# HGRN2 scores on the diagonal and between pair neighbours: two sets of keys in place of parity sums

## The chip, the cores and the metric

The kernel runs on one core of one Trainium2 chip, as one program. The metric is the device time of one execution in microseconds (us); lower is better. The engines go by the names of the profile: PE (TensorE matmuls), PEld (TensorE weight loads), DVE (VectorE), ACT (ScalarE), POOL (GpSimd) and SP, whose queue issues nearly all transfers from memory. Each engine takes its instructions strictly in the order in which the program wrote them; semaphores order them between engines.

## The reference

Two encoder layers over 512 tokens of width 1024 in float32. Each layer is a mixer and an expert-choice feed-forward network (FFN) with 16 experts. The mixer projects the normalised input onto nine groups of 512 columns, runs four retention heads and four HGRN2 heads of 128 channels, and projects back. What matters here is the HGRN2 head, in both directions over the sequence:

```
S_t = diag(f_t) S_{t-1} + k_t v_t^T        o_t = S_t^T q_t        k_t = 1 - f_t
scores[t, s] = sum_d q[t, d] k[s, d] prod_{s < r <= t} f[r, d]
```

The score of a token with itself is `sum_d q k`, with the keys of both directions added, since both include the diagonal. The score of a token with its neighbour in the same pair (tokens 2j and 2j+1) has a single forget factor, `sum_d q[t] k[s] f[t]`, from the forward direction for the later token and from the backward one for the earlier.

## The kernel before, in words

Channels lie on the 128 partitions and tokens along the free axis. For a head `c`, `K[:, hh]` holds the keys of both directions (2 x 512), `F[:, hh]` the forget factors and `self.q[:, c]` the queries. Scores inside a block of 128 tokens are made level by level: level width m = 1 joins tokens within a pair, and LEVELS = 2, 4, ..., 64 join ever larger neighbours. `ascend(c, n, m)` moves a head up one level: it multiplies half of the keys by forget products (DVE, L551, "kv" below), copies them to a tile for the next level's matmuls (two ACT copies, L531, "keys"), multiplies half of the queries (DVE, L556, "qv") and makes the products for the next level (POOL, L561). At each level four matmuls (L604) make scores of four blocks of 128 tokens, and DVE puts those that belong to the level into `AT` under a mask (L606).

The heads go in two pairs, (0, 1) and (2, 3). `hgrn_pair` is a generator: for both heads the keys of the two directions are added (POOL, L568) and Q = F q is made (DVE, L569); then the products for the diagonal and the neighbour (DVE, L579 and L580), which are split into a rounded part (ACT, L582) and a rest (POOL, L583); then `ascend(c, 0, 1)`; then four matmuls with `parity`, a matrix of alternating ones and zeros, sum the products over the channels (PE, L591), and DVE multiplies the sums by a mask of pairs (L594). After that come the levels, the transposes of the keys ("turn", L619), the states between blocks (L644, L647, L650) and the outputs (L663, copied out by ACT, L632). The float32 matmuls (L604, L644, L663, L721) each show as two loads and two matmuls in the trace; those of the reduced form fp32r (L465, L591) show as one.

The generator is woven into the projections by `lead`. A projection `proj(n, ...)` yields 16 times, after every six matmuls (L465; 128 x 512 each). At every yield a credit rises by the projection's budget B; while it is over zero, the generator is advanced to its next yield, whose value is taken off the credit. So the place of each HGRN step among PE's matmuls is fixed when the program is written:

```
credit += budget
while side is not None and credit > 0.0:
    cost = next(side, None)
    if cost is None:
        break
    credit -= cost
```

The budgets are 1.0, 1.2, 1.0, 0.9 and 2.2 for projections n = 3 to 7. In order they make `v2`, then `rq` and `rk`, which are rotated head by head in the last four yields of their projection (two ACT copies of half the partitions, L513 and L514; DVE L515; POOL L516; DVE L523, added one head late), then `rv` and `rg`. The yields' values stand in `COSTS`, with 1.2 for the Q step, 0.4 for a turn, 1.0 for states and 0.5 for outputs. Retention (L720, L721, its ACT copies L723, its states by the same L644) is added to the generator from n = 7 on. The weights of a projection are split into a rounded part and a rest as they are needed (ACT L436, DVE or POOL L438). The FFN's matmuls are L1145 and L1265; its weights are read from memory into the 22 slots of 1 MB that the mixer gives back when it is done, by DMAs that SP issues in one order.

Of the kernel before, what the change touches and what calls it, by code (L numbers as in the profile page):

```python
# [10 lines left out]
F32R = mybir.dt.float32r  # L11
BF = mybir.dt.bfloat16
U8 = mybir.dt.uint8
AF = mybir.ActivationFunctionType
OP = mybir.AluOpType

P = 128
S = 512
D = 1024
NT = S // P  # L20
# [45 lines left out]
class Kernel:  # L66
# [156 lines left out]
    def more_consts(self):  # L223
        nc, a, cp = self.nc, self.a, self.cp
        q = nc.gpsimd
        pt = self.pb()
        nc.tensor.transpose(pt[:, :24], self.rows, self.ident[:24, :24])
        for i in range(2):
            nc.tensor.transpose(pt[:, 24 + 8 * i:32 + 8 * i], self.rows2[:, self.apart(0, i)], self.ident[:8, :8])
        self.cols = cp.tile([P, 40], F32, name="cols")  # L230
        nc.vector.tensor_copy(self.cols[:, :24], pt[:, :24])

        nc.vector.tensor_copy(self.cols[:, 24:].rearrange("p (j two) -> p two j", two=2),
                              pt[:, 24:40].rearrange("p (two j) -> p two j", two=2))
        self.lmask = cp.tile([P, len(LEVELS), P], U8, name="lmask")
        lm = self.tmp4([len(LEVELS), P])
        q.dma_start(lm, a["lmask"])
        nc.gpsimd.tensor_copy(self.lmask, lm)
        for nm, shape in (("slots", [CAP]), ("sel", [NH + 1 + NT]), ("two", [P]), ("fold", [NE]), ("dec_k", [NH, 2])):
            t = cp.tile([P] + shape, F32, name=nm)  # L240
            setattr(self, nm, t)
            q.dma_start(t, a[nm])

        turns = self.tmp2(shape=(P + 2,))
        nc.gpsimd.memset(turns, 0.0)
        nc.gpsimd.memset(self.view(turns, 1, [[2, P // 2 + 1]]), 1.0)
        self.parity = cp.tile([P, P + 2], F32R, name="parity")
        nc.gpsimd.tensor_copy(self.parity, turns)
        self.selR = cp.tile([P, NH + 1], F32R, name="selR")
        nc.gpsimd.tensor_copy(self.selR, self.sel[:, :NH + 1])  # L250
        u = self.tmp2(shape=(P,))
        q.dma_start(u, a["upto"])
        self.upto, self.all = cp.tile([P, P], BF, name="upto"), cp.tile([P, P], BF, name="all")
        nc.gpsimd.tensor_copy(self.upto, u)
        nc.gpsimd.memset(self.all, 1.0)
        self.lower_bound()
# [159 lines left out]

    WAITS, RATE = (1, 1, 2), 0.7
    EARLY = 5
    COSTS = (1.2, 1.3, 0.65, 1.9)
    BUDGET = (1.0, 1.2, 1.0, 0.9, 2.2, 1.3)  # L420
    GROUPS = (4, 5, 6, 7, 0, 1, 2, 3, 8)

# [111 lines left out]
    def hgrn_pair(self, hp):  # L534

        nc, v = self.nc, self.nc.vector
        heads = (2 * hp, 2 * hp + 1)
        F, K = self.F[hp], self.K[hp]  # L540
        Q = self.slot([2, 2, S])
        AT, T, Tn, kt, B = {}, {}, {}, {}, {}

        def ascend(c, n, m):

            q0, k0, J = Q[:, c % 2], K[:, c % 2], S // (2 * m)
            t, ts = T[c]
            to = t.offset
            kv = self.view(k0, m, [[S - m, 2], [2 * m, J], [1, m]])
            tk = bass.AP(tensor=t.tensor, offset=to, ap=[list(t.ap[0]), [ts + 1, 2], [2, J], [0, m]])  # L550
            v.tensor_tensor(kv, kv, tk, op=OP.mult)  # L551
            if 2 * m < P:
                kt[c] = self.level_keys(B[c][:, n % 2], k0, 2 * m)
            qv = self.view(q0, 0, [[S + m, 2], [2 * m, J], [1, m]])
            tq = bass.AP(tensor=t.tensor, offset=to + 1, ap=[list(t.ap[0]), [ts - 1, 2], [2, J], [0, m]])
            v.tensor_tensor(qv, qv, tq, op=OP.mult)  # L556
            dst, ds = (Tn[c], J) if n % 2 == 0 else (F[:, c % 2], S)
            te = bass.AP(tensor=t.tensor, offset=to, ap=[list(t.ap[0]), [ts, 2], [2, J]])
            td = bass.AP(tensor=t.tensor, offset=to + 1, ap=[list(t.ap[0]), [ts, 2], [2, J]])
            dv = bass.AP(tensor=dst.tensor, offset=dst.offset, ap=[list(dst.ap[0]), [ds, 2], [1, J]])  # L560
            nc.gpsimd.tensor_tensor(dv, te, td, op=OP.mult)  # L561
            T[c] = (dst, ds)

        for c in heads:
            hh = c % 2
            B[c] = self.slot([4, S])
            AT[c], Tn[c] = B[c][:, 2], B[c][:, 3]
            nc.gpsimd.tensor_tensor(AT[c], K[:, hh, 0], K[:, hh, 1], op=OP.add)  # L568
            v.tensor_tensor(Q[:, hh], F[:, hh], self.q[:, None, c].to_broadcast([P, 2, S]), op=OP.mult)  # L569
            T[c] = (F[:, hh], S)  # L570
            yield 1.2
        X = {}
        for c in heads:


            q0, k0, x = Q[:, c % 2], K[:, c % 2], B[c][:, :2]
            X[c] = self.slot([2, 2, S], F32R)
            flat = lambda t: t.rearrange("p (j two) -> p j two", two=2)
            v.tensor_tensor(self.view(x, 0, [[2, S // 2], [S + 1, 2]]), flat(AT[c]), flat(self.q[:, c]), op=OP.mult)  # L579
            v.tensor_tensor(self.view(x, S, [[2, S // 2], [1 - S, 2]]), self.view(k0, 1, [[2, S // 2], [S - 1, 2]]),  # L580
                            self.view(q0, 0, [[2, S // 2], [S + 1, 2]]), op=OP.mult)
            nc.scalar.activation(X[c][:, 0], x, AF.Copy)  # L582
            nc.gpsimd.tensor_tensor(X[c][:, 1], x, X[c][:, 0], op=OP.subtract)  # L583
            yield self.COSTS[0]
        for c in heads:
            ascend(c, 0, 1)
            yield self.COSTS[1]
        for c in heads:
            sc = self.pb()
            for i in range(4):  # L590
                nc.tensor.matmul(sc, lhsT=self.parity[:, 1 - i % 2:1 - i % 2 + P], rhs=X[c][:, i // 2, i % 2],  # L591
                                 start=(i == 0), stop=(i == 3))
            AT[c] = AT[c].rearrange("p (b t) -> p b t", b=NT)
            v.tensor_tensor(AT[c], sc.rearrange("p (b t) -> p b t", b=NT),  # L594
                            self.two[:, None, :].to_broadcast([P, NT, P]), op=OP.mult)
            self.put(X[c])
            yield self.COSTS[2]
        for n, m in enumerate(LEVELS, 1):
            for c in heads:
                q0 = Q[:, c % 2]  # L600
                sc = self.pb().rearrange("p (b t) -> p b t", b=NT)
                for b in range(NT):
                    qv = self.view(q0, b * P, [[2 * m, P // (2 * m)], [S + m, 2], [1, m]])
                    nc.tensor.matmul(sc[:, b], lhsT=kt[c][:, b * P:(b + 1) * P], rhs=qv, start=True, stop=True)  # L604
                ascend(c, n, m)
                v.copy_predicated(AT[c], self.lmask[:, None, n - 1].to_broadcast([P, NT, P]), sc)  # L606
                yield self.COSTS[3]

        W = {}
        for c in heads:  # L610
            part = lambda x: x[:, :3 * P].rearrange("p (b t) -> p b t", b=3)
            W[c] = [part(B[c][:, 0]), part(B[c][:, 1]), part(F[:, c % 2, 0]), part(F[:, c % 2, 1])]
        for c in heads:
            hh = c % 2
            for d in range(2):
                pk = self.pb().rearrange("p (b t) -> p b t", b=NT)
                for i in range(3):
                    b = i + 1 - d
                    nc.tensor.transpose(pk[:, i], K[:, hh, d, b * P:(b + 1) * P], self.ident)  # L619
                nc.scalar.activation(W[c][d], pk[:, :3], AF.Copy)  # L620
            yield 0.4
        for c in heads:
            t, ts = T[c]
            self.states(W[c], self.v2, c, lambda d, b: t[:, d * ts + b:d * ts + b + 1])
            yield 1.0
        for c in heads:
            hh = c % 2
            if self.oh is None:
                self.oh = self.slot([NH, S])
            po = self.tile_outputs(W[c], self.v2, c, AT[c], Q[:, hh, 0, :3 * P], Q[:, hh, 1, P:])  # L630
            yield 0.5
            nc.scalar.activation(self.oh[:, c], po, AF.Copy)  # L632
            self.put(B[c])
        self.put(F, K, Q)
# [70 lines left out]
    def retention(self):  # L705
# [5 lines left out]
        nc.gpsimd.dma_start(dec_q, self.a["dec_q"])  # L711
        W, X, AT = {}, {}, {}

# [656 lines left out]
```

## Time and profile before

| what | value |
|---|---|
| three runs | 1638.16, 1639.77, 1640.24 us; median 1639.77 |
| the profiled execution | 1637.67 us, of which the span of its instructions is 1635.8 us |
| PE busy, PE weight loads busy | 94%, 58% of the span |
| DVE, ACT, POOL busy | 41%, 29%, 14% |
| mean granted TensorE clock | 0.977 of full speed |

The profile is of one execution, and its times are read against its own 1637.67 us. A busy share of PE counts matmuls from start to modelled end, which overlap; idle time of PE is listed as waits, with the instruction that ended each. The granted clock is given as a share of full speed (1.00 is 2.4 GHz, 0.50 is 1.2 GHz).

### The profile page before, as it was taken

To read this page: it belongs to the slowest core of one execution; us is meant where nothing else is said; L and a number is where in the kernel's file an instruction comes from. 1 tells how busy PE (TensorE), PEld (TensorE's weight loads), DVE (VectorE), ACT (ScalarE), POOL (GpSimd) and SP (SyncE) were. 2 spreads that over 40 slices of the span, in tenths; PEclk is the share of its full clock that TensorE was granted. 3 is DMA by queue.
4 is the path that set the end of the run, shared out by engine and by line. 5 is a ranking of instruction groups with operands and counts; after the bars stand their busy time and mean duration, and the time that the engine had idled before them with its cause. 6 is when DMAs were issued, how large, how long until landed. Compare 5 with 4: busy or idle time off the path is not lost. (4 is left out here: it accounts for less than half of the span.)

```text
span 1635.8 us, 19932 instructions
## 1 busy us (share of the span) xinstructions
PE 1531.0 (94%) x7970; PEld 954.9 (58%) x7970; DVE 664.4 (41%) x1107; ACT 474.9 (29%) x889; POOL 229.3 (14%) x201
## 2 busy tenths in 40 slices
PE   7989899969999999999999899999699999999986
PEld 6878798754354534533478787977444445444333
DVE  5378945561121312212254889464511122212113
ACT  4334444542221200200343434455322202112003
POOL 3042542100000000011021344430000000000201
PEclk9999999989999999999999999999799999999998
DMA  7211132577999999999941211317699999999997
GB/s 262 75 53 52 52 124 78 211 303 301 427 425 426 427 426 427 426 427 427 400 176 51 78 41 64 123 52 258 273 385 427 420 427 426 427 427 426 426 426 275
DMA packets 94605, 464.53 MB, mean 284 GB/s; under 512 B 7904, under 2 KB 16288, under 8 KB 48432
## 3 DMA queue, kind: packets, MB, share of 16 engines
q1 hardware_dynamic: 93040, 458.35, 69.0%
q0 software_dynamic: 1472, 4.90, 0.8%
q8 instruction: 63, 1.03, 0.2%
q14 instruction: 30, 0.25, 0.0%
HBM read 459.03 MB, written 4.19 MB: 283 GB/s over the span
## 5 line engine op out<-in xcount | busy, mean ns | idle before, releaser
L1145 PE MATMUL pj<-s,s 128*64 128x512 f32 x2048 | 478.8, 599 | 19.2 <-DMA s<-in_w_up_dram 13.9
L465 PE MATMUL pj<-s,s 128*128 128x512 f32 x1728 | 426.7, 401 | 12.9 <-DVE s L438 8.6
L465 PEld LDWEIGHTS pj<-s,s 128*128 128x128 f32 x1728 | 324.2, 192 | 82.7 <-DVE s L438 11.6
L1145 PEld LDWEIGHTS pj<-s,s 128*64 128x64 f32 x2048 | 173.3, 137 | 279.6 <-issue 203.3
L1265 PE MATMUL pb<-s,t 128*64 128x512 f32 x896 | 197.8, 594 | 5.4 <-ACT t L1183 2.7
L1272 POOL TENSOR_TENSOR s<-s,s 128x1024 f32<-128x1024 f32 x8 | 18.7, 2362 | 872.1 <-DVE s L1205 823.5
L1265 PEld LDWEIGHTS pb<-s,t 128*64 128x64 f32 x896 | 66.0, 137 | 126.8 <-issue 110.8
L1193 DVE SCALAR_TENSOR_TENSOR t<-pb,sm,t 128x512 fp32r<-128x512 f32 (+1 forms) x34 | 24.5, 719 | 242.5 <-ACT t L1192 241.0
L1205 DVE TENSOR_TENSOR s<-s,pb 128x512 f32<-128x512 f32 (+1 forms) x112 | 67.3, 661 | 130.0 <-PE pb L1200 130.0
L909 PE MATMUL pj<-s,s 128*128 128x512 f32 x384 | 96.6, 400 | 3.4 <-DVE s L796 2.9
L438 DVE TENSOR_TENSOR s<-s,s 128x1024 fp32r<-128x1024 f32 x62 | 84.3, 1383 | 37.8 <-ACT s L436 37.6
L1110 DVE COPY sm<-pb 128x2 f32<-128x2 f32 x16 | 2.5, 159 | 210.9 <-PE pb L1107 210.9
L909 PEld LDWEIGHTS pj<-s,s 128*128 128x128 f32 x384 | 69.3, 189 | 20.7 <-DVE s L796 4.6
L1192 ACT ACTIVATE t<-pb,sm 128x512 fp32r<-128x512 f32 (+1 forms) x34 | 22.5, 662 | 195.4 <-PE pb L1265 183.2
L1088 PEld LDWEIGHTS pb<-t,t 128*128 128x128 f32 x512 | 64.9, 199 | 17.3 <-issue 15.0
L1121 ACT ACTIVATE t<-pb 128x512 fp32r<-128x512 f32 x16 | 9.6, 601 | 221.0 <-PE pb L1119 221.0
L436 ACT ACTIVATE s<-s 128x1024 fp32r<-128x1024 f32 x72 | 73.4, 1048 | 0.0
L1088 PE MATMUL pb<-t,t 128*128 128x256 f32 x512 | 69.8, 293 | 3.2 <-DVE t L1072 2.4
L1200 PE MATMUL pb<-t,t 128*128 128x512 f32 (+1 forms) x256 | 66.7, 401 | 0.1
L556 DVE TENSOR_TENSOR s<-s,s 128x512 f32<-128x512 f32 x56 | 59.3, 1059 | 13.4 <-PE pb L604 13.4
L1200 PEld LDWEIGHTS pb<-t,t 128*128 128x128 f32 x256 | 44.7, 188 | 33.0 <-issue 19.4
L531 ACT ACTIVATE s<-s 128x256 f32<-128x256 f32 x96 | 35.3, 415 | 93.8 <-DVE s L551 93.5
(237 smaller groups left out, 1541.2 us busy)
## 6 DMA issues: line engine op xcount, KB each, us to landing
s<-in_w_gate_dram SPq DMA_DIRECT2D x124, 1024.0 KB, 19.5
s<-in_w_up_dram SPq DMA_DIRECT2D x124, 1024.0 KB, 19.6
s<-in_w_down_dram SPq DMA_DIRECT2D x112, 1024.0 KB, 19.6
s<-in_w_in_dram SPq DMA_DIRECT2D x34, 1024.0 KB, 5.9
s<-in_w_down_dram SPq DMA_DIRECT2D x32, 512.0 KB, 9.4
s<-in_w_out_dram SPq DMA_DIRECT2D x8, 1024.0 KB, 4.8
s<-in_x_dram SPq DMA_DIRECT2D x8, 512.0 KB
s<-in_w_gate_dram SPq DMA_DIRECT2D x8, 512.0 KB, 5.6
```

Source lines behind the costliest of these rows:

```text
L436: nc.scalar.activation(wh, src, AF.Copy)
L438: e.tensor_tensor(low, src, wh, op=OP.subtract)
L465: nc.tensor.matmul(pg[c], lhsT=lhsT, rhs=rhs, start=(k == 0 and m == 0), stop=(k == ND - 1 and m == 2))
L531: self.nc.scalar.activation(kv[:, :, e], src, AF.Copy)
L556: v.tensor_tensor(qv, qv, tq, op=OP.mult)
L909: nc.tensor.matmul(po, lhsT=x, rhs=w, start=(k == 0 and i == 0), stop=(k == ND - 1 and i == 2))
L1088: nc.tensor.matmul(pt[:, i], lhsT=x[:, tt, k % 2::2], rhs=oh[:, tt], start=(tt == 0 and x is self.picked[u][0]), stop=(tt == NT - 1 and x ...
L1145: nc.tensor.matmul(pg[n + 2 * f][e * CAP:(e + 1) * CAP], lhsT=self.xe[:, k, at + e * CAP:at + (e + 1) * CAP], rhs=w[e][:, f * 512:(f + 1) ...
L1193: v.scalar_tensor_tensor(yL[0][:, cs], py, gate, yH[0][:, cs], op0=OP.mult, op1=OP.subtract)
L1200: nc.tensor.matmul(pc, lhsT=ohT[:, tt * P:(tt + 1) * P], rhs=y[:, cs], start=(y is yH[0]), stop=(y is yL[0]))
L1205: v.tensor_tensor(dst, dst, pc, op=OP.add)
L1265: nc.tensor.matmul(py[f][e * CAP:(e + 1) * CAP], lhsT=hT[:, k, e * CAP:(e + 1) * CAP], rhs=W[e][:, k2, f * 512:(f + 1) * 512], start=(k == ...
```

## The change

The products, their split, and the matmuls with `parity` go, and so does `parity` itself. Instead each head gets two sets of keys in a tile `near`: set i serves the queries of parity i. At a token of the same parity it holds the sum of both directions' keys (POOL writes it there, strided), and at the other it holds the neighbour's key, already multiplied by its forget factor: `ascend(c, 0, 1)` makes it, and a new ACT copy brings it to `near`. Eight float32 matmuls per head (four blocks, two parities; 128 x 128 keys, 64 queries at every other token) then make the scores, and DVE multiplies by the same mask of pairs. One entry of COSTS (1.2, for the products) falls away, so that everything after it comes at an earlier yield.

```diff
-        turns = self.tmp2(shape=(P + 2,))
-        nc.gpsimd.memset(turns, 0.0)
-        nc.gpsimd.memset(self.view(turns, 1, [[2, P // 2 + 1]]), 1.0)
-        self.parity = cp.tile([P, P + 2], F32R, name="parity")
-        nc.gpsimd.tensor_copy(self.parity, turns)
...
-    COSTS = (1.2, 1.3, 0.65, 1.9)
+    COSTS = (1.3, 0.65, 1.9)
...
+        near = self.slot([2, 2, S])
+        flat = lambda t: t.rearrange("p (j two) -> p j two", two=2)
         for c in heads:
             hh = c % 2
             B[c] = self.slot([4, S])
-            AT[c], Tn[c] = B[c][:, 2], B[c][:, 3]
-            nc.gpsimd.tensor_tensor(AT[c], K[:, hh, 0], K[:, hh, 1], op=OP.add)
+            AT[c], Tn[c] = B[c][:, 2].rearrange("p (b t) -> p b t", b=NT), B[c][:, 3]
+            nc.gpsimd.tensor_tensor(self.view(near[:, hh], 0, [[2, S // 2], [S + 1, 2]]), flat(K[:, hh, 0]), flat(K[:, hh, 1]), op=OP.add)
             v.tensor_tensor(Q[:, hh], F[:, hh], self.q[:, None, c].to_broadcast([P, 2, S]), op=OP.mult)
             T[c] = (F[:, hh], S)
             yield 1.2
-        X = {}
         for c in heads:
-            q0, k0, x = Q[:, c % 2], K[:, c % 2], B[c][:, :2]
-            X[c] = self.slot([2, 2, S], F32R)
-            flat = lambda t: t.rearrange("p (j two) -> p j two", two=2)
-            v.tensor_tensor(self.view(x, 0, [[2, S // 2], [S + 1, 2]]), flat(AT[c]), flat(self.q[:, c]), op=OP.mult)
-            v.tensor_tensor(self.view(x, S, [[2, S // 2], [1 - S, 2]]), self.view(k0, 1, [[2, S // 2], [S - 1, 2]]),
-                            self.view(q0, 0, [[2, S // 2], [S + 1, 2]]), op=OP.mult)
-            nc.scalar.activation(X[c][:, 0], x, AF.Copy)
-            nc.gpsimd.tensor_tensor(X[c][:, 1], x, X[c][:, 0], op=OP.subtract)
+            ascend(c, 0, 1)
+            nc.scalar.activation(self.view(near[:, c % 2], 1, [[S - 1, 2], [2, S // 2]]),
+                                 self.view(K[:, c % 2], 1, [[S - 1, 2], [2, S // 2]]), AF.Copy)
             yield self.COSTS[0]
         for c in heads:
-            ascend(c, 0, 1)
+            sc = self.pb().rearrange("p (b t) -> p b t", b=NT)
+            for b in range(NT):
+                for i in range(2):
+                    nc.tensor.matmul(sc[:, b, i::2], lhsT=near[:, c % 2, i, b * P:(b + 1) * P],
+                                     rhs=self.q[:, c, b * P + i:(b + 1) * P:2], start=True, stop=True)
+            v.tensor_tensor(AT[c], sc, self.two[:, None, :].to_broadcast([P, NT, P]), op=OP.mult)
             yield self.COSTS[1]
-        for c in heads:
-            sc = self.pb()
-            for i in range(4):
-                nc.tensor.matmul(sc, lhsT=self.parity[:, 1 - i % 2:1 - i % 2 + P], rhs=X[c][:, i // 2, i % 2],
-                                 start=(i == 0), stop=(i == 3))
-            AT[c] = AT[c].rearrange("p (b t) -> p b t", b=NT)
-            v.tensor_tensor(AT[c], sc.rearrange("p (b t) -> p b t", b=NT),
-                            self.two[:, None, :].to_broadcast([P, NT, P]), op=OP.mult)
-            self.put(X[c])
-            yield self.COSTS[2]
+        self.put(near)
```

## Rows read from the trace of the kernel before

**Rows 1.** By stage: PE, PEld, DVE, ACT, POOL busy us; granted clock; DMA share, GB/s.
```profile
82.80:240.00 157.20, 148.30 (x829) 127.63 (x828) 118.27 (x145) 64.18 (x123) 68.97 (x62) 0.96 0.19 66
...
310.00:850.00 540.00, 509.01 (x2603) 260.33 (x2602) 147.98 (x313) 120.78 (x233) 19.25 (x11) 0.98 0.94 387
```

**Rows 2.** PE's waits, 75 to 240 us (layer 0): total, times, longest.
```profile
PE pb L591 <- POOL s L583: 4.5, 3, 2.2
PE pb L604 <- ACT s L531: 2.4, 1, 2.4
PE pj L465 <- DVE s L438: 2.0, 1, 2.0
```

**Rows 3.** PE's waits, 890 to 1070 us (layer 1); the L604 row repeats rows 2.
```profile
PE pb L591 <- POOL s L583: 4.6, 3, 2.3
...
PE pj L465 <- DVE s L438: 2.2, 1, 2.2
PE pb L591 <- ACT s L582: 1.0, 1, 1.0
```

**Rows 4.** Busy time in stretches at half clock (columns as in rows 1).
```profile
96.80:103.60 6.80, 4.84 (x12) 3.26 (x12) 6.80 (x5) 0.90 (x3) 5.43 (x3) 0.50 0.22 84
...
195.80:199.20 3.40, 3.40 (x12) 2.82 (x12) 3.40 (x3) 1.00 (x3) 3.05 (x2) 0.50 0.00 0
```

**Rows 5.** The chain that ended last, layer 1: start, us, what.
```profile
917.47 2.74 PE pj L465 x12
920.21 0.89 PE pb L604 x8
```

**Rows 6.** Groups by line and shape: busy us, mean ns, idle before.
```profile
L604 PEld LDWEIGHTS pb<-s,s 128*128 128x128 f32 x384 | 51.6, 194 | 10.3 <-ACT s L531 6.5
...
L531 ACT ACTIVATE s<-s 128x256 f32<-128x256 f32 x96 | 35.3, 415 | 93.8 <-DVE s L551 93.5
...
L583 POOL TENSOR_TENSOR s<-s,s 128x1024 fp32r<-128x1024 f32 x8 | 22.1, 2789 | 18.3 <-ACT s L582 14.8 <-issue 3.4
...
L1107 PEld LDWEIGHTS pb<-sm,t 128*64 128x64 f32 x256 | 15.2, 138 | 7.5 <-issue 7.5
...
L495 ACT ACTIVATE s<-pj 128x512 f32<-128x512 f32 x16 | 9.5, 592 | 19.2 <-PE pj L465 19.1
...
L723 ACT ACTIVATE s<-pb,dec_k 128x384 f32<-128x384 f32 x16 | 8.4, 578 | 6.9 <-PE pb L720 6.9
```

**Rows 7.** Timeline of the first pair's start, layer 0: start, us, engine, line.
```profile
79.58 2.58 DVE L569 TENSOR_TENSOR s<-s,s 128x1024 f32<-128x1024 f32 x2 [11.62 <-ACT s L477]
...
87.50 2.53 POOL L568 TENSOR_TENSOR s<-s 128x512 f32<-128x512 f32 x2
88.81 2.18 DVE L579 TENSOR_TENSOR s<-s,s 128x512 f32<-128x512 f32 x1 [6.65 <-POOL s L568]
...
93.72 0.63 PE L591 MATMUL pb<-s,parity 128*128 128x512 f32 x2
...
98.76 3.47 POOL L561 TENSOR_TENSOR s<-s 128x512 f32<-128x512 f32 x2
...
99.81 1.52 DVE L551 TENSOR_TENSOR s<-s,s 128x512 f32<-128x512 f32 x1
...
102.71 0.68 DVE L551 TENSOR_TENSOR s<-s,s 128x512 f32<-128x512 f32 x1
```

**Rows 8.** Timeline of one head's rotation in `rq`, layer 0.
```profile
145.15 0.59 ACT L513 ACTIVATE t<-pj 64x512 f32<-64x512 f32 x1
...
146.38 0.69 DVE L515 TENSOR_TENSOR s<-pj,t 128x512 f32<-128x512 f32 x1 [2.19 <-ACT t L514]
146.42 1.29 POOL L516 TENSOR_TENSOR t<-t,t 128x512 f32<-128x512 f32 x1 [1.57 <-ACT t L514]
146.98 1.28 DVE L523 TENSOR_TENSOR s<-s,t 128x512 f32<-128x512 f32 x1
```

More of the change, by code (lines that the diff above doesn't have):

```diff
@@ L606, in hgrn_pair @@
                 v.copy_predicated(AT[c], self.lmask[:, None, n - 1].to_broadcast([P, NT, P]), sc)
-                yield self.COSTS[3]
+                yield self.COSTS[2]
         W = {}
```

## Prediction

> **What bounds the kernel now.** I read the stages first [rows 1]. In the FFN the DMA engines are busy for 94% of the time, and its transfers can only begin when the mixer gives its slots back: during the HGRN stage the DMA share is 0.19. So a microsecond gained or lost in the mixer moves the whole FFN after it and comes out at the end one for one; the stage to look at is 82.8 to 240 us, and its like in layer 1. There PE is busy for 148.3 of 157.2 us while DVE is for 118.3 and POOL for 69.0. PE sets the time, and what it waits for is next.
>
> PE's waits in the two stages are few [rows 2, 3]: for the rest of the products (POOL L583) before the parity matmuls, 4.5 and 4.6 us; for a split that is late on DVE (L438), 2.0 and 2.2; for the products' rounded part (L582), 1.0 in layer 1; and, apart from the changed code, for level keys (L531), 2.4 each. Each batch of waits is followed by a stretch at half the clock, 1.2 GHz [rows 4]: in the 6.8 us one PE is busy for 4.84, and half of that, 2.4, is lost; in the 3.4 us ones, of which there are two per layer, it is busy throughout and loses 1.7. So the changed steps cost PE, beyond their own work, 6.5 + 7.8 of waiting and 2 x (2.4 + 1.7) of clock: 22.5 us in all. The level-key wait with its clock is another 4.1 per layer.
>
> **PE's own work.** Six L465 take half of 2.74 us [rows 5], so 0.228 each. The parity matmuls have the same form and size: four per head, 0.91. They go. The new ones are eight float32 matmuls per head, so 16 loads and 16 matmuls, of which the trace has the same kind with 128 moving columns: eight pairs in 0.89, 0.111 a pair [rows 5]. Do 64 columns halve that? A load of 128 columns lasts 194 ns and one of 64 lasts 138 [rows 6]: 0.87 ns per column, so 128 columns stream for about 0.11 us, the whole of a pair. The loads alone fill the pace, and I take 16 x 0.111 = 1.78 per head. That is 0.87 more than before, and with eight heads in two layers **+7.0**. If the moving columns set the pace it would be 0.89 per head and the change nothing (-0.2 in all); if load and matmul did not overlap, 0.111 + 0.056, 2.67 per head and +14.1.
>
> The Trainium skill says ("TensorE: Matmul & The Clock Gate", The mechanism) that a load overlaps a matmul in flight only when their row groups differ; by that rule the full 128-row loads here would be serial and the term +14.1. The trace speaks against it: eight pairs with loads of 0.11 and matmuls of the same length would then take 1.8 us, not 0.89 [rows 5].
>
> **Where the scores now stand.** I worked the credits through by hand. Before, the first pair's scores follow yields 8 and 9 of the `v2` projection, after 48 and 54 L465; two steps of 1.2 are gone, so now both heads' scores come together after yield 6, after 36. For the second pair the savings add up. Before: its Q steps at yield 16 of `rq` and 1 of `rk`, its scores at yield 7 of `rk`. After: Q at yields 13 and 14 of `rq`, `ascend` with the new copy at 15 and 16, both scores at yield 1 of `rk`. These are the four yields at which `rq` is rotated. Behind PE's scores stand all the matmuls of `rk`, so a wait there is lost.
>
> **First pair.** PE reaches the scores 12 x 0.228 = 2.7 us before the 93.72 at which it began the parity matmuls [rows 7], so at 91.0. The key sums (POOL L568) end at 90.03. While they run, DVE stands nearly still: L579 took 2.18, against some 1.1 that remained after POOL was done. Beside POOL's L561 a kv takes 1.52, and 0.68 without it [rows 7]. So the first head's kv ends at about 91.2, two key copies of 0.415 and the new copy of about 0.59 (L495, the same count) [rows 6] at 92.6, and PE waits 1.6. The second head's qv and kv follow qv of the first; near is complete about 95.0, PE is free at 92.6 + 1.78 = 94.4, and waits 0.6. With one half-clock stretch of 1.7 that makes 4.0 (2.2 without it, 5.6 with two). In layer 1, where the waits were 1.0 longer, I take 5.0. **+9.0.**
>
> **Second pair, the largest term.** Let zero be the moment when PE has the first head of `rq`. It then has one head's outputs left (L663, 20 pairs, 2.2) and four times six L465 (1.37): it reaches the scores at 7.7, and the second head's at 9.5. The others have more. ACT needs 1.2 per rotated head, DVE 0.69 for L515, POOL 1.29 for L516, DVE 0.67 to 1.28 for L523 [rows 8], in the order written: head 0, Q and sum, head 1, Q and sum, head 2, kv/keys/qv/copy, head 3, kv/keys/qv/copy. The last kv waits on DVE for 4 L515, 3 L523, 2 Q (1.29 each [rows 7]) and 2 of kv and qv: 2.8 + 2.0 + 2.6 + 1.4, and 0.7 for itself, from 1.3 on: 10.8, and with keys and copy 12.2. So even with POOL out of the way PE waits 2.7. POOL is not out of the way: L523 took 0.6 more beside L516 [rows 8], L579 1.1 more beside L568. Four L516, two sums and one L561 come to 5.2 + 2.5 + 1.7 = 9.4; if all of that holds DVE up, less 2.8 while L515 reads PSUM, which it did beside L516 in its usual 0.69, the last copy is done at 18.8, and 1.2 later still because ACT rotates head 3 only after the first head's copy: a wait of up to 10.5. The nearest rows show DVE held for most of an overlap, so I take 8.5 for both heads. After it I put 2.5 for the clock (1.7 for one stretch, up to 4). 11.0 per layer, **+22.0**; at the lower bound 4.4 per layer.
>
> The Trainium skill ("SBUF — State Buffer", Who interferes with whom) calls the port that DVE shares with POOL an exclusive lock for operations with two SBUF inputs. By it the wait would be the 10.5 and the term 26; the trace agrees for L523 and L579, and does not for kv beside L561, which went on at less than half pace.
>
> **What else shifts.** The level-key wait at the end of `rk` goes: the step whose keys were late was issued after all four rotations and used three yields on. Now the steps there are issued at yields 13 and 15, with four yields to their use. From the first rotated head on, the later kv has three L515, three L523 and one step of some 2.1 before it on DVE, after 1.2 on ACT: 9.9 with itself, its keys at 10.7. PE is there after six times 1.37 and three levels of 0.89, at 10.9. That is just in time, and for a DVE that is behind I give back 1.5 per layer (0 to 4.1, as before): -8.2 + 3.0, **-5.2**. The HGRN steps now end three yields before the end of `rv`, so retention's first yield holds the first head's keys and, with nothing between, its states, which need two ACT copies of 0.578 [rows 6] after the transposes: 1.4 per layer, **+2.8**, from nothing to 3. The rest I cost at nothing. The products' DVE work, and POOL's L583 (2.79 each [rows 6]), come off engines that nothing else waits for but the waits already counted. The matrix `parity` was made by POOL early in layer 0. Two slots fewer are held and one more; weights of projections are not among PE's waits [rows 2, 3].
>
> **Sum.** +7.0 - 22.5 + 9.0 + 22.0 - 5.2 + 2.8 = +13.1, on 1637.67 some 1650.8. The median of the runs is 2.1 above the profiled execution, so I say **1653**. With my own bounds on the second pair and on what remains at other places, the likeliest case spans about 1642 to 1664.
>
> **Rivals.**
> - The second pair's keys come in time. In its favour: POOL is rid of two L583 per pair, 5.6 us, and DVE of four products. Against it: four rotations stand in the same queues, and even the free chain is 2.7 late. At 1 us per layer in place of 11 the sum is -6.9: 1633. It decides from a second-pair cost of 4.4 per layer downwards: there the sum is about zero. Chance 0.14 for faster.
> - The waits move and balance. The second pair at its lower bound, 4.4 per layer, gives -0.1: no change, 1640. Or the FFN takes up the loss, against which the idle DMA in the mixer speaks. Chance 0.10.
> - Loads that don't overlap: +7.1 more, 1660. Pairs of 0.111 with loads as long speak against it. Chance 0.08.
> - The forecast, slower by the second pair's wait: 0.68.
>
> Slower 0.76, same (within 0.2%, about what a measurement of this kernel can tell from no change) 0.10, faster 0.14. The range reaches from the balance to a second pair at its upper bound with a clock loss of 4 (+7 above the forecast) and part of serial loads: **1638 to 1666**.
>
> **What would show it.** New matmuls at 0.11 a pair; no POOL waits of parity matmuls; the longest PE waits of the stage on the new ACT copy, two per pair, in the second pair next to L513 to L523; half-clock stretches after them; retention's first states waiting for L723; the wait for L531 at 195 us gone or shorter. Wrong it would be if the second pair's scores run without a wait of several microseconds, or if pairs with 64 columns take half the time.

## The result and the profile after

The changed kernel takes 1680.39 us (median of four runs, 1676.39 to 1682.72) where the kernel before takes 1639.08 on the same chip (four runs, 1638.16 to 1640.24): a ratio of 1.0249, 95% interval 1.0227 to 1.0271. That is slower, as forecast, but by 41 us in place of 13, and outside the range. The profiled execution after has a span of 1679.4 us, 43.6 longer than that of before.

First, by stage, where the 43.6 us are. The marks are the first matmuls of each stage in the two traces, and the end.

| stage | before, us | after, us | difference |
|---|---|---|---|
| start to the end of the layer 0 mixer's projections | 298.0 | 311.4 | +13.4 |
| output projection and selection, layer 0 | 72.3 | 72.5 | +0.2 |
| FFN, layer 0 | 451.3 | 459.1 | +7.8 |
| mixer, layer 1 | 285.5 | 297.9 | +12.4 |
| output projection and selection, layer 1 | 72.3 | 72.5 | +0.2 |
| FFN, layer 1, to the end | 456.4 | 465.9 | +9.5 |

The mixers lose 25.8 us and the FFNs 17.3. Nothing in the prediction has the second number: it let the FFN only follow the mixer.

The mixer first. PE's waits in layer 0 of the kernel after, 75 to 260 us (total, times, longest):
```profile
PE pb L579 <- ACT s L572: 9.9, 4, 5.9
PE pj L459 <- POOL s L432: 1.5, 1, 1.5
PE pb L630 <- ACT s L709: 1.0, 1, 1.0
PE pj L459 <- DVE s L509: 0.8, 1, 0.8
PE pb L590 <- ACT s L525: 0.6, 1, 0.6
```
L579 are the new score matmuls, L572 is the new ACT copy; the waits for the products are gone, and of the 2.4 for level keys of [rows 2] the 0.6 of the last row is left. In layer 1 the first row reads (900 to 1090 us; the four others are the same):
```profile
PE pb L579 <- ACT s L572: 11.4, 4, 5.9
```
The timeline shows the two pairs of layer 0 (start, us, engine, line; in brackets the idle time before it and what ended that):
```profile
92.59 2.00 PE L579 MATMUL pb<-s,s 128*128 128x64 f32 x16 [0.90 <-ACT s L572]
...
95.42 3.67 PE L579 MATMUL pb<-s,s 128*128 128x64 f32 x16 [0.82 <-ACT s L572]
...
155.35 1.75 POOL L566 TENSOR_TENSOR s<-s 128x512 f32<-128x512 f32 x1
155.87 2.31 DVE L567 TENSOR_TENSOR s<-s,s 128x1024 f32<-128x1024 f32 x1
...
158.70 1.15 DVE L517 TENSOR_TENSOR s<-s,t 128x512 f32<-128x512 f32 x1
159.26 1.48 POOL L555 TENSOR_TENSOR s<-s 128x512 f32<-128x512 f32 x1
159.77 1.52 DVE L545 TENSOR_TENSOR s<-s,s 128x512 f32<-128x512 f32 x1
...
162.05 0.64 ACT L572 ACTIVATE s<-s 128x512 f32<-128x512 f32 x1
...
162.74 3.67 PE L579 MATMUL pb<-s,s 128*128 128x64 f32 x16 [5.86 <-ACT s L572]
...
168.01 0.65 ACT L572 ACTIVATE s<-s 128x512 f32<-128x512 f32 x1
...
168.71 3.68 PE L579 MATMUL pb<-s,s 128*128 128x64 f32 x16 [2.30 <-ACT s L572]
```
The second pair waits 5.86 and 2.30, 8.16 in all, and behind DVE's queue: a Q product (L567), a rotation (L517), the kv (L545), all slowed beside POOL, then the keys and the copy on ACT. One score batch of 16 pairs lasts 2.00 at the full clock and 3.67 at the half.

Stretches of the kernel after, by the columns of [rows 1]; the three in the middle are those at half the clock, 1.2 GHz:
```profile
82.80:253.00 170.20, 156.40 (x871) 136.53 (x870) 105.31 (x137) 62.62 (x125) 57.32 (x58) 0.92 0.18 61
...
95.20:102.00 6.80, 6.58 (x25) 6.00 (x26) 3.11 (x4) 2.65 (x5) 0.00 (x0) 0.50 0.00 0
160.10:177.20 17.10, 12.16 (x48) 11.30 (x49) 9.64 (x11) 5.46 (x11) 4.99 (x5) 0.50 0.00 0
214.70:218.10 3.40, 3.20 (x12) 2.91 (x13) 2.85 (x5) 2.29 (x5) 0.40 (x2) 0.50 0.02 5
320.00:850.00 530.00, 496.75 (x2535) 244.83 (x2534) 135.91 (x300) 110.68 (x221) 16.18 (x9) 0.98 0.96 392
```
The stage's granted clock fell from 0.96 [rows 1] to 0.92. From within the second pair's first wait on, the clock is low for 17.1 us, not for the 3.4 or 6.8 of [rows 4]. Half of PE's busy time in each stretch is what the clock takes: 3.3, 6.1 and 1.6 us, 11.0 per layer, against 2.4 + 1.7 + 1.7 = 5.8 before.

Then the FFN. Its DMA engines are as busy as before (0.96 in the last row, 0.94 in [rows 1]; the windows of the two rows differ, so their GB/s do not compare) but, where they run without a break, they move less. The transfers of 450 to 780 us, inside the FFN of layer 0, in the kernel before:
```profile
DMA packets 19304, 140.71 MB, mean 426 GB/s; under 512 B 2142, under 2 KB 2142, under 8 KB 2142
```
and in the kernel after:
```profile
DMA packets 18988, 138.40 MB, mean 419 GB/s; under 512 B 2108, under 2 KB 2108, under 8 KB 2108
```
The same 8 KB packets are moved at 419 in place of 426 GB/s. One packet's record lasts 313 ns (median; mean over this stretch 315.1) in place of 309 (309.6). At an FFN bound by its transfers, 315.1 / 309.6 of 907.7 us is +16.1, which is about the whole of its +17.3.

What in the diff can slow a packet? The removed matrix `parity` stood in the pool of constants, ahead of the slots. Its 520 bytes per partition, with padding 544, are gone, so every slot starts 544 bytes lower: the first at byte 7648 of a partition in place of 8192 (these bytes are those of the kernels' layout; the traces show no addresses). The slots are what the FFN's weights are loaded into.

### The profile page after: what moved, and what is told of

It is laid out like the page before. It is cut to its first block, busy times and chain, and to the rows that moved or that the text cites. A ratio compares the mean times of both kernels' runs of the same rounds, so it can differ in the third digit from the quotient of the medians.

```text
span 1679.4 us, 20079 instructions
## 1 busy us (share of the span) xinstructions
PE 1559.0 (93%) x8066; PEld 970.7 (58%) x8066; DVE 636.6 (38%) x1091; ACT 471.6 (28%) x889; POOL 204.2 (12%) x190
## 5 line engine op out<-in xcount | busy, mean ns | idle before, releaser
L459 PE MATMUL pj<-s,s 128*128 128x512 f32 x1728 | 428.1, 401 | 10.8 <-POOL s L432 3.0
L1131 PEld LDWEIGHTS pj<-s,s 128*64 128x64 f32 x2048 | 169.1, 137 | 291.7 <-issue 207.6
L432 DVE TENSOR_TENSOR s<-s,s 128x1024 fp32r<-128x1024 f32 x62 | 77.6, 1275 | 52.8 <-ACT s L430 52.4
L1107 ACT ACTIVATE t<-pb 128x512 fp32r<-128x512 f32 x16 | 9.6, 601 | 225.9 <-PE pb L1105 225.9
L1152 ACT ACTIVATE t<-pj,sm 128x512 f32<-128x512 f32 x32 | 22.0, 687 | 141.5 <-PE pj L1131 141.5
```

The costliest lines, as they stand in the source:

```text
L432: e.tensor_tensor(low, src, wh, op=OP.subtract)
L459: nc.tensor.matmul(pg[c], lhsT=lhsT, rhs=rhs, start=(k == 0 and m == 0), stop=(k == ND - 1 and m == 2))
L1131: nc.tensor.matmul(pg[n + 2 * f][e * CAP:(e + 1) * CAP], lhsT=self.xe[:, k, at + e * CAP:at + (e + 1) * CAP], rhs=w[e][:, f * 512:(f + 1) ...
```

## Experiments

All kernels of a group ran on one chip beside the kernel before (1639.04, 1640.55 and 1639.62 us). Mixer times below are from the first projection matmul to the last, layer 0 and layer 1: before 282.6 and 285.5, after 296.1 and 297.9. FFN times are those of the table.

### Where the slots start

**The change with the slots back at 8192.** A pad of the freed size is all that is added:
```diff
+        nc.gpsimd.memset(cp.tile([P, 136], F32, name="pad"), 0.0)
         self.selR = cp.tile([P, NH + 1], F32R, name="selR")
```


> The changed kernel with an unused tile of 544 bytes in the place that parity had, so that the slots begin at byte 8192 again. Theory (start of the slots): the FFN stages go back to 451 and 456 us, the mixers keep their 13.4 and 12.4 us of loss, the time is 1662 to 1666. Rival (the whole loss comes from the mixer): 1677 to 1683.

Measured: 1664.62 us, ratio 1.0154 [1.0137, 1.0171], 15.8 below the changed kernel. The packets are back at 309 ns, the FFNs at 452.4 and 459.3, the mixers at 294.1 and 298.0. The same stretch of transfers:
```profile
DMA packets 19299, 140.67 MB, mean 426 GB/s; under 512 B 2142, under 2 KB 2142, under 8 KB 2142
```

**The kernel before with its slots moved to 7648.** Nothing but the place of the matrix is changed:
```diff
-        self.parity = cp.tile([P, P + 2], F32R, name="parity")
+        self.parity = self.sm.tile([P, P + 2], F32R, name="parity", tag="parity", bufs=1)
```


> The kernel before with its tile of parity moved to another pool behind the slots, so that the 22 slots begin at byte 7648 of each partition, as they do in the changed kernel, in place of 8192; computation, order and schedule stay. Theory (the FFN's transfers slow down because the slots' start moved): the two FFN stages get 8 and 10 us longer, as they did with the change, 8 KB packets take 313 ns in place of 309, and the time is 1655 to 1658. Rival (the FFN's loss comes from the mixer's change, or differs from one loading of a program to the next): 1637 to 1641.

Measured: 1653.23 us, ratio 1.0088 [1.0073, 1.0104]: 14.2 us slower with the old scores, a little under the 1655 to 1658 expected and far from the rival. Packets 313 ns, FFNs 457.6 and 464.4 (+6.3 and +8.0), mixers 283.2 and 285.9. The transfers:
```profile
DMA packets 18985, 138.38 MB, mean 419 GB/s; under 512 B 2107, under 2 KB 2107, under 8 KB 2107
```
So the place of the slots alone costs 14 to 16 us, in either kernel.

**Which starts are good?** Two pads of other sizes in the changed kernel.
```diff
+        nc.gpsimd.memset(cp.tile([P, 24], F32, name="pad"), 0.0)   # slots at 7744
+        nc.gpsimd.memset(cp.tile([P, 72], F32, name="pad"), 0.0)   # slots at 7936
```


> The changed kernel with an unused tile of 96 bytes among the constants: the slots begin at 7744, a multiple of 64 and not of 256. If a start off a multiple of 256 costs the same wherever it is off, 8 KB packets take 313 ns as at 7648 and the kernel some 1680 us. If a multiple of 64 is enough, 309 ns and some 1664 us. If the cost grows with the distance, 310 to 311 ns and some 1668 us.

> The changed kernel with an unused tile of 288 bytes: the slots begin at 7936, a multiple of 256 and not of 512. If 256 is what counts, packets take 309 ns and the kernel some 1664 us; if 512 or more is needed, 313 ns and some 1680 us.

Measured: 1674.47 with the start at 7744, 1662.5 with it at 7936 (one run each). FFNs 457.0 and 464.3 for the first, 451.2 and 458.8 for the second; packets 312 and 309 ns. At 7744 (a multiple of 64, not of 256):
```profile
DMA packets 19050, 138.88 MB, mean 421 GB/s; under 512 B 2111, under 2 KB 2111, under 8 KB 2111
```
At 7936, which is 31 x 256:
```profile
DMA packets 19298, 140.66 MB, mean 426 GB/s; under 512 B 2142, under 2 KB 2142, under 8 KB 2142
```
7648 and 7744 are slow, 7936 and 8192 fast: of these four, the fast ones are the multiples of 256 bytes. They are also the multiples of 128; a start at a multiple of 128 that is none of 256 was not tried. The time at 7744 fits neither the 1680 nor the 1668 expected: the FFNs take 3.7 us less than at 7648, and the first mixer, whose half-clock stretches are shorter in this run, some 3.5 less. The Trainium skill says ("DMA: Bandwidth & Descriptors", How a descriptor splits into AXI transactions) that a transfer is cut into pieces of 256 bytes that must start at multiples of 256, and that the first piece of one which starts between them begins at the multiple below. The runs agree with it in which starts are slow; for 8 KB it would be an estimated 33 pieces for 32, 3%, where the packets grew by 1.8% in their mean. The page counts pieces of reads, while here it is the destination in SBUF that moved. No trace shows the pieces.

### What the second pair's wait costs

**The wait filled.** In the aligned kernel, PE is given matmuls to do where it waited in the second pair: 24 before the first head's scores, 17 before the second's, into a PSUM tile that nothing reads.
```diff
+            if hp:
+                idle = self.pb()
+                for i in range((24, 17)[c % 2]):
+                    nc.tensor.matmul(idle, lhsT=self.xH[0][:, 0, :P], rhs=self.xH[0][:, i % 4], start=True, stop=True)
             for b in range(NT):
```


> As the changed kernel with aligned slots, but in the second pair PE runs 24 and 17 matmuls of 512 columns, whose sums nobody reads, before the first and the second head's scores, where it would wait. Theory (of the second pair's loss, the wait is one part and the half clock that lasts for 17 us from it on the other): the clock stays at 1.2 GHz for at most 3.4 us there and the waits shrink below 1 us each, the keys come no sooner; the kernel is faster than with aligned slots alone by some 8 us (2 layers x 6.0 lost to the clock, less 1.8 that the slow scores hid in the wait), 1654 to 1658. Rival (the clock costs little, the wait is all): no faster, 1662 to 1668.

Measured: 1657.07 us, ratio 1.0111 [1.0096, 1.0126], 7.6 below the aligned kernel although PE does no useful work in the place of the wait. The stretch of 150 to 180 us (columns as in [rows 1]) in the changed kernel, and then with the wait filled:
```profile
150.00:180.00 30.00, 21.84 (x99) 19.23 (x99) 19.59 (x20) 10.71 (x21) 14.90 (x11) 0.72 0.10 36
```
```profile
150.00:180.00 30.00, 29.51 (x158) 24.84 (x157) 22.48 (x26) 10.27 (x21) 14.11 (x12) 1.00 0.21 71
```
The granted clock goes from 0.72 to 1.00, and no half-clock stretch is left behind the second pair. That part of the clock loss is thus the wait's doing. PE in the place of the wait:
```profile
154.69 5.60 PE L580 MATMUL pb<-s 128*128 128x512 f32 x24
160.76 2.00 PE L584 MATMUL pb<-s,s 128*128 128x64 f32 x16 [0.47 <-ACT s L573]
162.56 4.15 PE L580 MATMUL pb<-s 128*128 128x512 f32 x17
```
Not all of the 2 x 6.1 us comes back: the filling matmuls (L580), 5.60 and 4.15 us from first start to last end (0.36 of it beside the matmuls before them), with the 0.47 that PE still waits, outlast the 8.16 they replace by some 1.7 per layer, and two new waits of 0.53 and 0.72 for DVE come up in `rk`. Two stretches elsewhere changed too: the 3.4 us at the end of `rk` is gone in both layers, although the waits of 0.8, 1.5 and 0.6 before it are still there, and behind the first pair of layer 1 the clock is low for 10.2 us in place of 6.8.

**The steps spread out.** The scheduler is told that each of the new key steps costs 2.5 in place of 1.3; the scores of the second pair then come after yield 7 of `rk`, where they were in the kernel before.
```diff
-    COSTS = (1.3, 0.65, 1.9)
+    COSTS = (2.5, 0.65, 1.9)
```


> As the changed kernel with aligned slots, but the step with ascend and the new copy has the value 2.5 in place of 1.3, so that scores and everything behind them stand where they stood before. Theory (PE waits for the new copies because the scores come too early, the second pair's in the midst of the rotations of rq): no wait of PE for the new copy over 1 us, the parity matmuls' waits and their half-clock stretches gone too, PE's own work +7: 1639 - 22.5 + 7, some 1621 to 1630. Rival (the longer chain through ascend and the copy makes the wait wherever the scores stand): the waits of 2 to 6 us per pair stay, 1650 to 1664.

Measured: 1621.69 us, ratio 0.9895 [0.9881, 0.991]: 42.9 below the aligned kernel and 17.4 below the kernel before. Mixers 274.3 and 276.0. PE's waits in layer 0, 75 to 260 us:
```profile
PE pb L591 <- ACT s L526: 2.0, 1, 2.0
PE pj L460 <- DVE s L433: 1.7, 1, 1.7
PE pj L460 <- POOL s L433: 1.1, 1, 1.1
```
(lines are one higher than after). None is for the new copy; in layer 1 there is one for it, of 0.5. The same 30 us as above:
```profile
150.00:180.00 30.00, 30.00 (x169) 26.13 (x168) 23.11 (x27) 11.61 (x22) 11.39 (x9) 1.00 0.22 71
```
No half-clock stretch stands in the mixers' HGRN part, in either layer.

**The first pair alone, and the second alone.**
```diff
-            yield self.COSTS[0]
+            yield self.COSTS[0] + 1.2 * (1 - hp)     # first pair alone
+            yield self.COSTS[0] + 1.2 * hp           # second pair alone
```


> As with aligned slots, but the step with ascend and the new copy has the value 2.5 in the first pair alone and 1.3 in the second. So the second pair starts where it did before, behind the rotations of rq, and its scores come 3 and 4 yields into rk, 3 and 2 yields sooner than in the paced kernel. Theory (the rotations make the second pair's copies late; clear of them they are done 8.2 and 9.4 us after rk begins, as in the paced kernel): one wait of 2 to 3 us for the first head's copy, none for the second's, at most 3.4 us at half clock there; 1624 to 1633. Rival (what counts is how many yields lie between copy and scores, wherever they stand): waits near the 8.2 us of the change, 17 us at half clock, 1640 to 1656.

> The change with the aligned slots, and 2.5 in place of 1.3 in the second pair's key steps alone. If the scores' place decides, they come after yields 4 and 5 of rk, as in the run with the first pair slowed, so PE still waits 1.5 to 3 us there once per layer, and the first pair keeps its waits and its half clock (some 5 us per layer): 1642 to 1652. Rival, the gains of the two slowed pairs simply add up (42.9 for both, 25.2 for the first alone, 17.7 left): 1645 to 1648 with no wait of over 1 us before the second pair's scores and no half clock after it.

Measured, first pair alone: 1639.46 us, ratio 0.9994 [0.9984, 1.0005], 6 us above the range of the theory and just below its rival's. Mixers 281.4 and 284.3. The waits for the copy are as expected, one of 2.5 per layer with 3.4 us (layer 1: 6.8) at half clock, and in layer 1 one of 0.5 in the first pair; what the expectation lacked are the others (layer 0, 75 to 260 us):
```profile
PE pb L580 <- ACT s L573: 2.5, 1, 2.5
PE pb L650 <- DVE s L637: 1.6, 1, 1.6
PE pj L460 <- POOL s L433: 1.5, 1, 1.5
PE pb L631 <- ACT s L710: 0.9, 1, 0.9
PE pb L591 <- ACT s L526: 0.8, 2, 0.6
PE pj L460 <- DVE s L510: 0.8, 1, 0.8
```
Over the whole mixer PE is idle for 8.8 us against 4.9 with both pairs slowed, and 1.7 go to the clock; 1.5 of the 7.1 us between the two kernels in layer 0 stay unplaced.

Second pair alone: 1653.0 us, ratio 1.0079 [1.0064, 1.0094], 1 us above the theory's range. Its waits in layer 0:
```profile
PE pb L580 <- ACT s L573: 5.4, 4, 2.2
PE pb L591 <- ACT s L526: 1.8, 1, 1.8
PE pj L460 <- POOL s L433: 1.1, 1, 1.1
```
Two of the four are the first pair's old 0.91 and 0.82; the second pair's are 2.24 and 1.46, and the clock is low for 13.7 us from the end of the first of them on, with PE busy for 12.24 of it. The gains of the two halves (26.7 and 12.2, each set against the kernel before on its own chip) do not add up to the 42.9 of both: slowing the first pair also moves the second pair's scores, and one half leaves the second pair a place where it still waits. By the count of PE's matmuls these scores follow yield 1 of `rk` in the changed kernel, 3 and 4 with the second pair slowed (one sooner than expected), 4 and 5 with the first slowed (one later), and 7 with both.

**The kernel before, spread out likewise.** Is it the pacing alone?
```diff
-    COSTS = (1.2, 1.3, 0.65, 1.9)
+    COSTS = (2.0, 1.3, 0.65, 1.9)
```


> The kernel before, with 2.0 in place of 1.2 for each of its four product steps per layer, so that the parity matmuls come about two yields later. If pacing alone makes the gain of the slowed kernel, PE's waits for the products (9.1 us in both layers), most of the 2.2 to 2.4 us waits and their half clock go: 1620 to 1630. Rival, the change is needed for it, because the products keep POOL and DVE busy and the later steps of the second pair collide with the end of rk and retention: 1633 to 1645, with waits of similar sum at other lines.

Measured: 1644.82 us, ratio 1.0028 [1.0018, 1.0037]: slower, as the rival had it. PE's waits in layer 0:
```profile
PE pj L465 <- DVE s L438: 4.2, 2, 2.2
PE pj L465 <- POOL s L438: 2.1, 2, 1.5
PE pb L604 <- ACT s L531: 1.0, 2, 0.6
PE pj L465 <- DVE s L515: 0.8, 1, 0.8
```
The waits for the products are down from 4.5 [rows 2] to 0.3, but those for the splits (L438), which share POOL and DVE with the products, rose from 2.0 to 6.3. At this one setting pacing gives the old scores nothing; other settings were not tried.

## Why the prediction was right and wrong

**Right: the bound and the sign.** PE sets the mixer's time, and the second pair's wait makes the kernel slower. Spreading the steps, which takes that wait away, makes it faster than before.

**Right: the price of the new matmuls.** 16 pairs take 2.00 us with the last one's end, 0.112 from start to start at the full clock, where 0.111 was taken; 64 moving columns do not halve it. That the 128-column loads set the pace fits L1107 of the kernel before, whose matmuls with 64-column loads and 2 moving columns start 0.058 apart (median). The rule of the Trainium skill that the prediction cites ("TensorE: Matmul & The Clock Gate", The mechanism), by which such loads wait for the matmul in flight, would make it 2.67 with loads of 0.11 [rows 6]: the trace does not agree with it here.

**Right: the waits.** Second pair 8.16 for 8.5 per layer, at the place and behind the queue that was named. First pair 0.90 + 0.82 for 2.2, in layer 1 2.39 + 0.81 for 3.2. Retention 0.97 for 1.4. The waits that were to go are gone but for the 0.56 for level keys; with it the end of `rk` kept 0.79 + 1.51 + 0.56 = 2.86 in place of 1.5: +2.7 for both layers.

**Right in size, by luck in part: the 8.5.** It was set between 2.7 and 10.5 on the reading that DVE, held up by POOL, still goes on at less than half pace. That reading is wrong. Each L545 and L517 of the changed kernel that began while a POOL operation ran ended 0.54 to 0.55 us after that operation, whether the two had overlapped for 0.15 or for 2.3 us (34 cases; above, L545 ends at 161.29 and POOL's L555 at 160.74); alone, L545 takes 0.68. The kv of [rows 7], 1.52 beside the first of two L561, ends 0.55 after that one too. The prediction cites the Trainium skill ("SBUF — State Buffer", Who interferes with whom) for an exclusive lock and says that the trace does not agree for kv. The trace agrees for kv as well. The wait stayed below the 10.5 because POOL and DVE met less than assumed: from 150 to 168 us DVE's operations took some 4.8 us longer than alone, where that bound had 9.4 - 2.8 = 6.6. Two slips of 0.1 in the working, 1.1 for the 0.97 us that L579 had left when POOL was done and 4.0 for 2.2 + 1.7, change nothing.

**Wrong: the step "After it I put 2.5 for the clock".** This term of the sum was mis-sized, in three places. After the second pair 6.1 us are lost, not 2.5; after the first pair 3.3, not 1.8; and at the end of `rk`, where the sum had no clock loss left, 1.6. In layer 1 the three stretches have the same lengths and lose 6.0, 3.2 and 1.6. That is 11.0 and 10.8 us where the sum had 4.3 per layer: +13.2. The upper bound of 4 was too low as well: it was read from stretches behind waits of 2 us [rows 4], and nothing in that trace shows one behind a wait of 5.9 followed by one of 2.3. The filled wait shows that the stretch hangs on the wait.

With +13.2 for the clock, +2.7 for `rk`, -0.7 and -0.5 for the second and the first pairs' waits and -0.9 for retention's, the forecast +13.1 becomes +26.9. One wait more shrank that the sum did not have: PE's last for a split in `rv`, 1.7 per layer before (at 267 us, behind the stretch of [rows 2]) and 0.4 after, -2.6. That makes +24.3, against the measured 25.8 of the two mixers.

**Wrong: the step "The rest I cost at nothing ... The matrix `parity` was made by POOL early in layer 0".** It looked at the time in which the matrix is made and not at the place it takes. Its removal moved the slots to a start at which the FFN's packets take 313 ns. That is 14 to 16 us, shown from both sides, by the old kernel with moved slots and the new one with its slots back. With its slots back the change takes 1664.62 us, 25.6 more than the kernel before beside it and inside the range that was given: this step put the result outside it, and the clock took it to the upper end.

**Left open.** Some 4 us of the FFNs' +17.3 remain with the slots aligned (+1.1 and +2.9, one profile each); in the other changed kernels whose slots start at 8192 the FFNs take 450.6 to 452.1 and 457.0 to 457.9, and at 7936 451.2 and 458.8, so part of it differs from one kernel to the next. Of the rivals, the pace of overlapping loads and the keys that come too late are settled as above; the FFN took up none of the loss.

## What to carry to other kernels

When a tile is added to or taken from the pools, look at where the tiles behind it now start, above all those that large transfers write: here 544 bytes cost more than the change's matmuls. When work is taken out of a stage whose steps a scheduler places by their costs, what follows moves forward; check what it now waits for, and set the costs anew before judging the change, which here turned +1.5% into -1.1%. A wait of several microseconds on TensorE should be priced with the clock it takes afterwards. Here that was 6.1 us behind 8.16 us of waiting and also 6.1 behind 2.24 and 1.46, so it does not shrink in step with the wait.

## What the runs showed of the hardware that was not expected

A slot start that is a multiple of 256 bytes (7936, 8192) or not (7744, 7648) makes 309 against 312 or 313 ns for an 8 KB packet and 426 against 421 or 419 GB/s.

The DVE products L517 and L545 (two SBUF inputs each), when begun while POOL was at work, ended 0.55 us after POOL's operation, however long the two had overlapped (0.15 to 2.3 us), as is told above.

The length of a half-clock stretch does not follow from one wait alone. Behind 5.86 and 2.30 us of waiting it was 17.1 us in both layers of the changed kernel, but 13.7 in layer 0 of the two kernels with the starts at 7744 and 7936; behind 2.24 and 1.46 (in layer 1 2.24 and 1.76) it was 13.7; behind a single wait of 2.5 it was 3.4 in one layer and 6.8 in the other; behind 0.90 and 0.82, 6.8 in the changed kernel and 3.4 with its slots aligned. What sets it was not tried.
